# FFN activations and conv's input moved by 64 bytes, FFN and conv products taken by token halves, a separate home for a tail's third weights

## The chip, the cores and the metric

The kernel runs on one core of a Trainium2 chip, in one launch. The metric is the device time of the whole launch in microseconds (us); a value is the median of several executions. A profile of one further execution gives the start and the duration of every instruction on each engine: TensorE (PE, with its weight loads as PEld), VectorE (DVE), ScalarE (ACT), GpSimd (POOL) and SyncE (SP).

## The reference, cut to what matters

A trunk of two layers over 512 tokens of width 1024. Each layer is FFN, mixer, FFN; the first mixer is a gated short convolution, the second a sparse attention. Each of the six sublayers has its own norm with shift, scale and gate.

```python
def adaln(x, g, shift, scale):
    return rms_norm(x, g) * (1 + scale[:, None, :]) + shift[:, None, :]

def swiglu(h, w_in, w_out):                     # D_FF = 2816
    g, u = jnp.split(h @ w_in, 2, axis=-1)
    return (jax.nn.silu(g) * u) @ w_out

def short_conv_mixer(h, w_in, conv_w, w_out):
    b_gate, c_gate, v = jnp.split(h @ w_in, 3, axis=-1)
    u = c_gate * v
    y = lax.conv_general_dilated(u, ...)        # width 3, depthwise, causal
    return (b_gate * y) @ w_out

for i in range(DEPTH):                          # DEPTH = 2
    h = adaln(x, norm_g[i, 0], shift[:, 0], scl[:, 0])
    x = x + HALF * gate[:, 0, None, :] * swiglu(h, ffn_w_in[i, 0], ffn_w_out[i, 0])
    h = adaln(x, norm_g[i, 1], shift[:, 1], scl[:, 1])
    y = short_conv_mixer(...) if i % 2 == 0 else nsa_mixer(...)
    x = x + gate[:, 1, None, :] * y
    h = adaln(x, norm_g[i, 2], shift[:, 2], scl[:, 2])
    x = x + HALF * gate[:, 2, None, :] * swiglu(h, ffn_w_in[i, 1], ffn_w_out[i, 1])
```

## The kernel before

Everything is held transposed: `x[d]` is one block of 128 channels by 512 tokens (d = 0 to 7). Every operand of a matmul is split into a high and a low part, so that a product of one weight block and one block of tokens is three matmuls, in `mm3`: L190 (high weights, high data), L191 (high weights, low data), L192 (low weights, high data). ScalarE rounds a tile to its high part and VectorE subtracts for the low part (`split`, L186 and L187). `HALVES` are the token ranges 0 to 256 and 256 to 512; `HT` is 256.

An FFN (`ffn`, four calls) works through its 22 blocks of the hidden width in four parts (`FOUR`). The input products `gu` are 256 tokens wide: most hidden blocks go through `seven_products`, a scheme with seven instead of eight products on sums and differences of blocks of the input (`th`, `tl`) and of the weights (`qa`, `qb`), whose split weights lie in the pool `sw`. The result of each block is activated and kept as `ahi`, `alo` in the pool `fa` of the class `Hidden`. After each of the first three parts its output products `y` follow: for each d, all blocks of the part, 512 tokens wide (L668), and VectorE adds the result to `x[d]`. The fourth part is the tail: products `ty` by token halves, of six d first, without the last hidden block at first (L695 to L701), then the rest; VectorE adds each to `x` (L408), ScalarE squares it (L271), VectorE sums the squares (L273).

When the sum over all d is complete for a token half, `finish` runs the norm: a small product (L290), `nv` (L292), an inverse square root in ten small VectorE steps `rs_...` (L219 to L233), a diagonal `dg` (L297), and a product that spreads it over the partitions (`pr`, L298). `piece` (L355 to L358) then makes the next layer's input `hhi`, `hlo`, on which the first products of the next layer run (`head_start`, tile `hs`).

The tail's weights are loaded for two d at a time, `ws`, four pairs of tiles: for d = 0 to 3 in the general weights pool (`whi`, `wlo`), for d = 4, 5 and d = 6, 7 in the places of `th2`, `tl2` and of `th0`, `tl0` in the pool `tt`, whose sums are no longer needed.

In `conv` 4 of the 24 blocks of the input product run first, as head start by token halves (`hs`, 192 matmuls); the other 20 are `cv`, 512 tokens wide (480 matmuls).

Where tiles start in on-chip memory is set by the pools: they are stacked from both ends in the order in which they are opened, and `shift(pool, n)` puts n bytes of filler into a pool. The order of instructions on each engine is decided by a scheduler when the program is built, from the order of the code and the priorities (`high_priority`, `issue_after`); an engine then runs its own list in that order.

Of the kernel before, what the change touches and what calls it, by code (L numbers as in the profile page):

```python
# [14 lines left out]
F32R = mybir.dt.float32r  # L15
# [7 lines left out]
P = 128  # L23
D = 1024
T = 512
HT = T // 2
KD = D // P
# [22 lines left out]
HALVES = ((0, HT), (HT, T))  # L50
# [3 lines left out]
def decoder_kernel(ctx, tc, xT, cT, ng, adaw, adab, ffi, ffo, cwi, cw, cwo,  # L54
# [3 lines left out]
    def pool(es, name, bufs, **kw):  # L58
        kw.setdefault("reuse_waits", "tile")
        return es.enter_context(tc.tile_pool(name=name, bufs=bufs, **kw))  # L60


    def shift(p, n):
        p.tile([P, n // 4], F32, name="shift")
# [12 lines left out]
    def psum(name, tag="mm"):  # L77
        tag = next(six) if tag == "mm" else {"pr": "o"}.get(tag, tag)
        return ps.tile([P, T], F32, name=name, tag=tag, bufs=2)
# [36 lines left out]
    for c in range(D // T):  # L116
        o = psum("cb", "nat")
# [3 lines left out]
    def mod(s, kind, d):  # L121
        c = s * NMOD + kind * KD + d
        return mods[:, c:c + 1]
# [65 lines left out]
    def mm3(o, sh, sl, mh, ml, first, last):  # L189
        nc.tensor.matmul(o, sh, mh, start=first, stop=False)  # L190
        nc.tensor.matmul(o, sh, ml, start=False, stop=False)  # L191
        nc.tensor.matmul(o, sl, mh, start=False, stop=last)  # L192

    def weights(src, nk, ncol, own=None, held=3, raws=None, to=None):
        def part(name, dt, bufs, from_):
            return (from_ or wp).tile([P, nk * ncol], dt, name=name, tag=name, padded_shape=[P, KD * P], bufs=bufs)

        held = held if own else 3
        hi, lo = to or (part("whi", F32R, held, own), part("wlo", F32R, held, own))
        raws = raws or own  # L200
        raw = part("wraw", F32, 3 if raws in (None, wp) else 2, raws)
        nc.sync.dma_start(raw.rearrange("p (a n) -> p a n", a=src.shape[1]), src)
        split(raw, hi, lo)
        return [t.rearrange("p (k n) -> p k n", n=ncol) for t in (hi, lo)]


    def project(o, w, wc, h, ks, first, last, a=0, b=T):
        c = slice(wc * P, (wc + 1) * P)
        for n, (kw, k) in enumerate(ks):
            mm3(o, w[0][:, kw, c], w[1][:, kw, c], h[0][k][:, a:b], h[1][k][:, a:b],  # L210
                first and n == 0, last and n == len(ks) - 1)
# [26 lines left out]
    class Halves:  # L238
        def __init__(self, *t):
            self.t = t  # L240
# [226 lines left out]

    class Hidden:
        def __init__(self, es, bufs):
            self.fa = pool(es, "fa", bufs, side="right")  # L470
            self.hi, self.lo = [], []

# [59 lines left out]
    def ffn(s, f, nrm, nxt, w0, ahead, extra=(), soon=()):  # L532
        with ExitStack() as es:
            first = s == 0
            hp = pool(es, "hp", 1)
# [88 lines left out]
                keep(e[:, 0:2].rearrange("p a b -> p (a b)"))  # L624

            js = [(j, c) for j in range(nj) for c in range(2)]
            shift(pool(es, "gap", 1, side="right"), 448)
            tt = pool(es, "tt", 1, side="right")
            if first:
                opening(f, nrm, hid, hp, tt, soon)  # L630
# [4 lines left out]
            else:  # L635
                with ExitStack() as tf_es:
                    nrm.alloc_seven(hp, pool(tf_es, "tf", 1))
                    h = nrm.hi, nrm.lo
                    with ExitStack() as hw_es:
                        hw = pool(hw_es, "hw", 1)  # L640
                        shift(hw, 64)
                        w = w0 + [weights(ffi[f, j, c], KD, P, hw, 1, wp) for j, c in js[len(w0):]]

                        to = [tt.tile([P, D], F32R, name="w" + e, tag=f"t{e}1") for e in "hl"]
# [14 lines left out]
            for p, (j0, j1) in enumerate(FOUR):  # L659
                for j in range(max(j0, nj), j1):  # L660
                    seven_products(j)
                n = j1 - j0
                a = (hid.hi[j0:j1], hid.lo[j0:j1])
                if p < len(FOUR) - 1:
                    for d in range(KD):
                        w = ffn_out(f, d, 1, j0, j1)
                        o = psum("y")
                        project(o, w, 0, a, [(k, k) for k in range(n)], True, True)  # L668
                        added = nc.vector.scalar_tensor_tensor(x[d], o, mod(s, 2, d), x[d], op0=ALU.mult, op1=ALU.add)
                        with tc.issue_after(added.ins):  # L670
                            each()
            assert not todo
            sw_es.close()


            ws = []
            for i, d in enumerate(range(0, KD, 2)):
                if i < 2:
                    ws.append(ffn_out(f, d, 2, j0, j1))
                else:  # L680
                    t = (2, 0)[i - 2]
                    to = [tt.tile([P, KD // 2, HT], F32R, name=f"t{e}{t}").rearrange("p a b -> p (a b)") for e in "hl"]
                    raw = (own if first or i == 2 else quarter[0])().rearrange("p a b -> p (a b)")
                    nc.sync.dma_start(raw.rearrange("p (a n) -> p a n", a=2),
                                      ffo[f, d:d + 2, :, j0 * P:j1 * P].rearrange("d p c -> p d c"))
                    split(raw, *to)
                    ws.append([t.rearrange("p (k n) -> p k n", n=P) for t in to])
# [14 lines left out]
            for d, t in [(d, 0) for d in range(6, KD)] + [(d, HT) for d in range(KD)]:  # L702
                o = psum("ty")
# [6 lines left out]
    def conv(s, nrm, nxt, extra, w0, ahead, own):  # L710
        with ExitStack() as es:
            h_es = es.enter_context(ExitStack())
            hp = pool(h_es, "hp", 1)
            shift(hp, 256)
            ca = pool(es, "cva", 2, side="right")
            h = nrm.alloc(hp)
            ks = [(k, k) for k in range(KD)]
            zh, zl = [], []

            table = bias_table(pool(h_es, "bt", 1))  # L720
            for n in (1, 12, 17):
                extra.insert(n, lambda: next(table, None))
            each = spread(extra, 4 * KD + KD - 3)

            def fill(ins, n):
                with tc.issue_after(ins.ins):
                    for _ in range(n):
                        each()
            for d in range(KD):
                if d == 0:  # L730
                    w = w0 + [weights(cwi[3], KD, P, own)]
                    *os, nx = head_start(nrm, h, [(lambda k, w=w_: (w, 0, k)) for w_ in w])
                else:
                    os = [nx] if d == 1 else []
                    for c in range(len(os), 3):
                        with behind(*nrm.done[0]) if d == 1 else nullcontext():
                            w = weights(cwi[3 * d + c], KD, P, own if (d + c) % 2 else None)
                        o = psum("cv")
                        project(o, w, 0, h, ks, True, True)
                        os.append(o)  # L740
                cg, v, b = os
                cs = tmp("cs")
                nc.scalar.activation(cs, cg, AF.Copy)
                u = ca.tile([P, T + 2], F32, name="u")
                nc.vector.memset(u[:, 0:2], 0.0)
                nc.vector.tensor_mul(u[:, 2:], cs, v)
                y = tmp("yc")
                nc.vector.tensor_scalar(y, u[:, 2:], cws[:, 2 * KD + d:2 * KD + d + 1], None, op0=ALU.mult)
                for i in (1, 0):
                    nc.vector.scalar_tensor_tensor(y, u[:, i:i + T], cws[:, i * KD + d:i * KD + d + 1], y,  # L750
                                                   op0=ALU.mult, op1=ALU.add)
                z = tmp("z")
                nc.vector.tensor_mul(z, y, b)
                hi = ca.tile([P, T], F32R, name="zhi", bufs=KD)
                lo = ca.tile([P, T], F32R, name="zlo", bufs=KD)
                _, rest = split(z, hi, lo)
                zh.append(hi)
                zl.append(lo)
                fill(rest, 4)
            z = (zh, zl)  # L760
            h_es.close()
            tw = pool(es, "tw", 1, side="right")
            for d in range(KD - 3):
                w = weights(cwo[d], KD, P)
                o = psum("y")
                project(o, w, 0, z, ks, True, True)
                fill(residual(s, d, o, nxt), 1)
            assert not extra
            return tail(s, nxt, [(d, weights(cwo[d], KD, P, tw), 0, ks) for d in range(KD - 3, KD)], z, ahead)
# [591 lines left out]
    w = ffn(0, 0, nrm, nxt, None, lambda: [weights(cwi[c], KD, P) for c in range(3)], [small] + late(2), soon)  # L1361
    nrm, nxt = nxt, Norm(2)
    with ExitStack() as ada_es:
        ap = pool(ada_es, "ada", 2)
        home = rows_in(ap)
        w = conv(1, nrm, nxt, [partial(j, home) for j in upto(4, -6)], w, ffn_ahead(1), ap)
    nrm, nxt = nxt, Norm(3)
    w = ffn(2, 1, nrm, nxt, w, ffn_ahead(2), late(5, -3))
    nrm, nxt = nxt, Norm(4)
    w = ffn(3, 2, nrm, nxt, w, lambda: nsa_in(4), late(6))  # L1370
    cd_es.close()
    nrm, nxt = nxt, Norm(5)
    w = nsa(4, nrm, nxt, w, ffn_ahead(3))
# [76 lines left out]
```

## Time and profile before

| | |
|---|---|
| median of 3 runs | 1926.12 us (1925.61 to 1926.36) |
| the profiled execution | 1924.62 us |
| its span | 1922.8 us |
| granted TensorE clock | 1.0 |
| first FFN: tail starts, last `ty` starts | 349.93, 373.27 us |
| second FFN: tail starts | 874.88 us |
| last FFN: tail starts | 1896.17 us |

The span runs from the first to the last instruction that the profile shows; the execution's own time is 1.8 us longer. Times in rows count from the start of the span. A row of the timeline has the start, the duration, the engine, the line of the code, the operation, the tile written and those read, the shapes, a count of instructions that are drawn together, and in brackets how long the engine stood idle before and what ended it. Matmuls are pipelined: a row's duration covers its way through the array, and the next one starts earlier than it ends.

### The profile page before, as it was taken

What the parts mean: (1) busy time and instruction counts of PE and PEld (TensorE: products, weight loads), DVE (VectorE), ACT (ScalarE), POOL (GpSimd) and SP (SyncE); (2) the same over time, 40 slices, a digit from 0 to 9 for tenths busy, and PEclk for the clock granted to TensorE, in tenths of its full rate; (3) what the DMA queues carried; (4) which work ended last, traced back from release to release, by engine and by line L of the source; (5) the groups of instructions that cost most, each with busy time, mean ns of one, the idle gap of its engine ahead of it and who ended that gap; (6) DMA issues with size and microseconds to landing.
All of it is one profiled execution on the core that took longest, in us unless ns stands there. A gap on an engine that the chain in (4) does not pass through costs nothing.

```text
span 1922.8 us, 34307 instructions
## 1 busy us (share of the span) xinstructions
PE 1881.2 (98%) x13321; PEld 1734.8 (90%) x13321; DVE 1584.4 (82%) x2771; ACT 898.7 (47%) x1471; POOL 247.9 (13%) x346
## 2 busy tenths in 40 slices
PE   6999999999999999999999999999999999999999
PEld 4989899988899899999989999999888789898989
DVE  8979888887788798888878888886898988685965
ACT  3435343432245343435634344464787756353532
POOL 0011110000011111110111110000354520010100
PEclk9999999999999999999999999999999999999999
DMA  8587666366656677663667765134322225564731
GB/s 317 193 263 193 217 175 222 124 223 248 227 162 184 210 187 244 173 224 110 173 221 187 230 177 190 63 138 123 98 74 70 89 61 149 153 178 129 187 106 65
DMA packets 126879, 325.07 MB, mean 169 GB/s; under 512 B 15435, under 2 KB 16203, under 8 KB 126716
## 3 DMA queue, kind: packets, MB, share of 16 engines
q1 hardware_dynamic: 95628, 244.13, 37.3%
q0 software_dynamic: 31088, 78.76, 17.8%
q8 instruction: 104, 1.70, 0.3%
q14 instruction: 59, 0.48, 0.1%
HBM read 314.18 MB, written 3.15 MB: 165 GB/s over the span
## 4 chain that ended last, share of the span: by engine, by line
PE 82%; DVE 8%; issue 3%; DMA 3%; POOL 2%; ACT 1%; SPq 1%; DVEq 0%; POOLq 0%; ACTq 0%
PE gu L192 12%; PE gu L190 12%; PE gu L191 12%; PE y L190 7%; PE y L191 6%; PE y L192 6%; PE hs L192 2%; PE hs L191 2%; PE hs L190 2%; PE cv L190 2%; PE cv L191 2%; PE cv L192 2%; PE ty L191 2%; PE ty L192 2%; PE ty L190 2%
## 5 line engine op out<-in xcount | busy, mean ns | idle before, releaser
L186 ACT ACTIVATE whi<-wraw 128x1024 fp32r<-128x1024 f32 (+1 forms) x268 | 262.0, 982 | 397.2 <-PE y L191 188.3
L187 DVE TENSOR_TENSOR wlo<-wraw,whi 128x1024 fp32r<-128x1024 f32 (+1 forms) x268 | 303.3, 1135 | 30.3 <-ACT whi L186 29.6
L190 PE MATMUL y<-ahi,whi 128*128 128x512 f32 x576 | 223.9, 392 | 1.2 <-ACT ahi L186 1.2
L192 PE MATMUL y<-ahi,wlo 128*128 128x512 f32 x576 | 222.8, 390 | 0.6 <-DVE wlo L187 0.6
L191 PE MATMUL y<-alo,whi 128*128 128x512 f32 x576 | 222.9, 390 | 0.0
L141 DVE CUSTOM_DVE_ANT_0 adaraw<-adaraw,cond 128x1024 f32<-128x1024 f32 x144 | 174.0, 1225 | 34.8 <-DMA adaraw<-in_adaw 34.7
L192 PE MATMUL gu<-hhi,wlo 128*128 128x256 f32 x728 | 201.4, 277 | 0.0
L190 PE MATMUL gu<-hhi,whi 128*128 128x256 f32 x728 | 201.4, 277 | 0.0
L191 PE MATMUL gu<-hlo,whi 128*128 128x256 f32 x728 | 201.3, 277 | 0.0
L567 POOL DMA_DIRECT2D qa<-in_ffi x70 | 84.6, 1209 | 691.7 <-DMA qa<-in_ffi 206.2
L192 PE MATMUL gu<-th,qal 128*128 128x256 f32 x584 | 161.4, 276 | 0.7 <-DVE qal L187 0.7
L190 PE MATMUL gu<-th,qah 128*128 128x256 f32 x584 | 161.5, 277 | 0.3 <-ACT p L611 0.3
L191 PE MATMUL gu<-tl,qah 128*128 128x256 f32 x584 | 161.3, 276 | 0.0
L191 PE MATMUL gu<-tl,qbh 128*128 128x256 f32 x584 | 161.3, 276 | 0.0
L192 PE MATMUL gu<-th,qbl 128*128 128x256 f32 x584 | 161.3, 276 | 0.0
L190 PE MATMUL gu<-th,qbh 128*128 128x256 f32 x584 | 161.3, 276 | 0.0
L190 PEld LDWEIGHTS gu<-hhi,whi 128*128 128x128 f32 x728 | 136.7, 188 | 0.5
L191 PEld LDWEIGHTS gu<-hlo,whi 128*128 128x128 f32 x728 | 136.6, 188 | 0.5
L192 PEld LDWEIGHTS gu<-hhi,wlo 128*128 128x128 f32 x728 | 136.7, 188 | 0.1
L186 ACT ACTIVATE qbh<-a 128x512 fp32r<-128x512 f32 x73 | 46.2, 633 | 188.4 <-PE gu L191 172.3
L190 PEld LDWEIGHTS y<-ahi,whi 128*128 128x128 f32 x576 | 107.3, 188 | 27.0 <-ACT ahi L186 5.8
L191 PEld LDWEIGHTS y<-alo,whi 128*128 128x128 f32 x576 | 108.1, 188 | 24.0 <-DVE alo L187 2.2
(320 smaller groups left out, 5602.3 us busy)
## 6 DMA issues: line engine op xcount, KB each, us to landing
wraw<-in_ffi SPq DMA_DIRECT2D x103, 512.0 KB
adaraw<-in_adaw POOLq DMA_DIRECT2D x77, 512.0 KB, 4.4
qa<-in_ffi SPq DMA_DIRECT2D x146, 256.0 KB
wraw<-in_ffo SPq DMA_DIRECT2D x96, 384.0 KB
qa<-in_ffi POOLq DMA_DIRECT2D x70, 512.0 KB, 7.0
adaraw<-in_adaw SPq DMA_DIRECT2D x67, 512.0 KB
a<-in_ffi SPq DMA_DIRECT2D x73, 256.0 KB
wraw<-in_cwi SPq DMA_DIRECT2D x24, 512.0 KB
```

The source lines that it names most:

```text
L141: nc.vector.tensor_tensor_reduce(out=raw, in0=raw, in1=cond, scale=1.0, scalar=0.0, op0=ALU.mult, op1=ALU.add, accum_out=m)
L186: act = nc.scalar.activation(hi, src, AF.Copy)
L187: return act, nc.vector.tensor_tensor(lo, src, hi, ALU.subtract)
L190: nc.tensor.matmul(o, sh, mh, start=first, stop=False)
L191: nc.tensor.matmul(o, sh, ml, start=False, stop=False)
L192: nc.tensor.matmul(o, sl, mh, start=False, stop=last)
L567: nc.gpsimd.dma_start(qa, bass.AP(tensor=a21.tensor, offset=a21.offset, ap=[a21.ap[0], [0, 2], a21.ap[1]]), accum_op=ALU.add)
```

## The change

Four edits. The filler of 448 bytes is put ahead of the pool `fa` instead of behind it, so that `ahi` and `alo` begin 64 bytes into a line of 128, and `tt` stays where it was. The `y` products of d = 1 to 7 are made in two halves of 256 tokens each, that of d = 0 in one as before. The tail's weights for d = 4, 5 get a pool of their own, `held`, on the other side, after `sw` is closed and where its first tiles were; those for d = 6, 7 take the place of `th2`, `tl2`. Conv's input begins 64 bytes into a line of 128 and its `cv` products are made by halves.

```diff
     class Hidden:
         def __init__(self, es, bufs):
+            shift(pool(es, "gap", 1, side="right"), 448)
             self.fa = pool(es, "fa", bufs, side="right")
...
             js = [(j, c) for j in range(nj) for c in range(2)]
-            shift(pool(es, "gap", 1, side="right"), 448)
             tt = pool(es, "tt", 1, side="right")
...
                         o = psum("y")
-                        project(o, w, 0, a, [(k, k) for k in range(n)], True, True)
+                        for t0, t1 in HALVES if d else ((0, T),):
+                            project(o[:, t0:t1], w, 0, a, [(k, k) for k in range(n)], True, True, t0, t1)
...
             sw_es.close()
-
+            es_ws = es.enter_context(ExitStack())
+            held = pool(es_ws, "held", 1)
+            shift(held, 64)
...
                 else:
-                    t = (2, 0)[i - 2]
-                    to = [tt.tile([P, KD // 2, HT], F32R, name=f"t{e}{t}").rearrange("p a b -> p (a b)") for e in "hl"]
+                    if i == 2:
+                        to = [held.tile([P, D], F32R, name="w" + e) for e in "hl"]
+                    else:
+                        to = [tt.tile([P, KD // 2, HT], F32R, name=f"t{e}2").rearrange("p a b -> p (a b)") for e in "hl"]
...
             hp = pool(h_es, "hp", 1)
-            shift(hp, 256)
+            shift(hp, 320)
...
                         o = psum("cv")
-                        project(o, w, 0, h, ks, True, True)
+                        for a, b in HALVES:
+                            project(o[:, a:b], w, 0, h, ks, True, True, a, b)
```

The scheduler orders the engines anew around these edits. Three places follow; names carry the tile numbers of their program.

TensorE in the second FFN, at the start of the first `y` products that follow a part of seven-product blocks; `y_7515` and `y_8504` belong to d = 0, `y_7544` and `y_8533` to d = 1, and `ahi_7505`, `ahi_8494` are the last hidden block of the part. Before:

```order
L192 MATMUL y_7515<-ahi_7380,wlo_7510 128x512
L190 MATMUL y_7544<-ahi_6880,whi_7538 128x512
L191 MATMUL y_7544<-alo_6881,whi_7538 128x512
L192 MATMUL y_7544<-ahi_6880,wlo_7539 128x512
L190 MATMUL y_7515<-ahi_7505,whi_7509 128x512
L190 MATMUL y_7544<-ahi_7005,whi_7538 128x512
L191 MATMUL y_7544<-alo_7006,whi_7538 128x512
L191 MATMUL y_7515<-alo_7506,whi_7509 128x512
```

And after:

```order
L192 MATMUL y_8504<-ahi_8369,wlo_8499 128x512
L190 MATMUL y_8533<-ahi_7869,whi_8527 128x256
L191 MATMUL y_8533<-alo_7870,whi_8527 128x256
L192 MATMUL y_8533<-ahi_7869,wlo_8528 128x256
L190 MATMUL y_8533<-ahi_7994,whi_8527 128x256
L191 MATMUL y_8533<-alo_7995,whi_8527 128x256
L190 MATMUL y_8504<-ahi_8494,whi_8498 128x512
L192 MATMUL y_8533<-ahi_7994,wlo_8528 128x256
```

Between the 15 products of d = 0 on earlier blocks and the first one on the last block stood three matmuls of 512 columns; now five of 256 stand there. The same holds at 11 of the 12 starts of `y` products, all but the first.

TensorE in the second FFN's tail, where its first half turns to the last hidden block (`ahi_9225`, `alo_9226` before, `ahi_10466`, `alo_10467` after). The tiles `ty_9272`, `ty_9273` and `ty_10517`, `ty_10518` belong to d = 0 and 1, `ty_9277` to d = 5, `ty_10520` to d = 3, `ty_10521` to d = 4. Before:

```order
L192 MATMUL ty_9277<-ahi_9100,tl2_9243 128x256
L190 MATMUL ty_9272<-ahi_9225,whi_9230 128x256
L191 MATMUL ty_9272<-alo_9226,whi_9230 128x256
L192 MATMUL ty_9272<-ahi_9225,wlo_9231 128x256
L190 MATMUL ty_9273<-ahi_9225,whi_9230 128x256
L191 MATMUL ty_9273<-alo_9226,whi_9230 128x256
```

And after:

```order
L192 MATMUL ty_10520<-ahi_10341,wlo_10482 128x256
L190 MATMUL ty_10517<-ahi_10466,whi_10475 128x256
L191 MATMUL ty_10517<-alo_10467,whi_10475 128x256
L192 MATMUL ty_10517<-ahi_10466,wlo_10476 128x256
L190 MATMUL ty_10518<-ahi_10466,whi_10475 128x256
L191 MATMUL ty_10518<-alo_10467,whi_10475 128x256
L192 MATMUL ty_10518<-ahi_10466,wlo_10476 128x256
L190 MATMUL ty_10519<-ahi_10466,whi_10481 128x256
L190 MATMUL ty_10521<-ahi_10091,wh_10487 128x256
L191 MATMUL ty_10521<-alo_10092,wh_10487 128x256
```

Six d had their nine matmuls on earlier blocks ahead of that point before, 54 in all; now four have, 36, and the products of d = 4 and 5 with the `held` weights (`wh`) come behind the first products on the last block.

VectorE in the first FFN's tail, from `nv` of the first token half on (`pr_3860`, `pr_4242`). Before:

```order
L292 TENSOR_SCALAR nv_3863<-pr_3860 128x2
L187 TENSOR_TENSOR wlo_3714<-wraw_3715,whi_3713 128x1024
L408 SCALAR_TENSOR_TENSOR x2_84<-ty_3921,mods_117,x2_84 128x256
L273 TENSOR_TENSOR nacc_3789<-nacc_3789,sq_3918 128x256
L219 TENSOR_SCALAR rs_i_3865<-nv_3863 128x2
L408 SCALAR_TENSOR_TENSOR x3_85<-ty_3938,mods_117,x3_85 128x256
L273 TENSOR_TENSOR nacc_3789<-nacc_3789,sq_3935 128x256
L221 TENSOR_SCALAR rs_j_3867<-rs_i_3865 128x2
L224 SCALAR_TENSOR_TENSOR rs_a_3869<-rs_j_3867 128x2
L187 TENSOR_TENSOR wlo_3720<-wraw_3721,whi_3719 128x1024
```

And after:

```order
L292 TENSOR_SCALAR nv_4245<-pr_4242 128x2
L219 TENSOR_SCALAR rs_i_4247<-nv_4245 128x2
L221 TENSOR_SCALAR rs_j_4249<-rs_i_4247 128x2
L224 SCALAR_TENSOR_TENSOR rs_a_4251<-rs_j_4249 128x2
L225 TENSOR_TENSOR rs_b_4252<-rs_a_4251,nv_4245 128x2
L226 SCALAR_TENSOR_TENSOR rs_r0_4253<-rs_b_4252,rs_j_4249 128x2
L408 SCALAR_TENSOR_TENSOR x1_83<-ty_4286,mods_117,x1_83 128x256
L229 TENSOR_TENSOR rs_a_4257<-rs_r0_4253 128x2
L230 TENSOR_SCALAR rs_r1_4259<-rs_r0_4253 128x2
L231 TENSOR_TENSOR rs_b_4258<-rs_a_4257,nv_4245 128x2
L232 SCALAR_TENSOR_TENSOR rs_a_4260<-rs_b_4258 128x2
```

The steps of the inverse square root stood apart, with two weight splits and residuals between the first four of them; now they follow each other, with one residual between.

## The prediction

> **What bounds the kernel now.** First the head of the page, then the chain that ended last.
>
> ```profile
> span 1922.8 us, 34307 instructions
> PE 1881.2 (98%) x13321; PEld 1734.8 (90%) x13321; DVE 1584.4 (82%) x2771; ACT 898.7 (47%) x1471; POOL 247.9 (13%) x346
> PE 82%; DVE 8%; issue 3%; DMA 3%; POOL 2%; ACT 1%; SPq 1%; DVEq 0%; POOLq 0%; ACTq 0%
> ```
>
> TensorE is busy 98% of the span and holds 82% of the chain, so what counts is the distance from one matmul's start to the next and the few places where TensorE waits. The durations in the rows are no distances, since matmuls overlap (a 128x512 one shows 0.39 us and the next starts after 0.23); I read distances from the timeline, as start of the last minus start of the first, over the count. Four places carry the argument. First the first and the last row of 18 steps through one `y` product, then of 84 steps through the `gu` products with `hhi`, and the same 84 in another place:
>
> ```profile
> 204.02 0.39 PE L190 MATMUL y<-ahi,whi 128*128 128x512 f32 x1
> 208.10 0.39 PE L190 MATMUL y<-ahi,whi 128*128 128x512 f32 x1
> 62.73 0.28 PE L190 MATMUL gu<-hhi,whi 128*128 128x256 f32 x1
> 72.25 0.28 PE L190 MATMUL gu<-hhi,whi 128*128 128x256 f32 x1
> 1859.40 0.28 PE L190 MATMUL gu<-hhi,whi 128*128 128x256 f32 x1
> 1868.97 0.28 PE L190 MATMUL gu<-hhi,whi 128*128 128x256 f32 x1
> ```
>
> 4.08 us / 18 = 226.7 ns at width 512; 9.52 / 84 = 113.3 ns at width 256, half of it to 0.1 ns; in the worse place 9.57 / 84 = 113.9 ns. Then the tail of an FFN: 18 steps with the first weights, 11 with the later ones, and conv's head start:
>
> ```profile
> 349.93 0.28 PE L190 MATMUL ty<-ahi,whi 128*128 128x256 f32 x1
> 352.09 0.28 PE L190 MATMUL ty<-ahi,whi 128*128 128x256 f32 x1
> ...
> 371.97 0.28 PE L190 MATMUL ty<-ahi,th 128*128 128x256 f32 x1
> 373.27 0.28 PE L192 MATMUL ty<-ahi,tl 128*128 128x256 f32 x1
> 374.49 0.70 PE L298 MATMUL pr<-dg,ones 128*128 128x256 f32 x2 [0.94 <-DVE u L745]
> 376.30 0.73 PE L190 MATMUL hs<-hhi,whi 128*128 128x256 f32 x4 [0.43 <-ACT hhi L357]
> 376.97 0.38 PE L191 MATMUL hs<-hlo,whi 128*128 128x256 f32 x1
> 400.04 0.40 PE L190 MATMUL cv<-hhi,whi 128*128 128x512 f32 x1
> ```
>
> 2.16 / 18 = 120.0 ns for `ty` on `whi`, 1.30 / 11 = 118.2 ns for `ty` on `th`. From 376.97 to 400.04 TensorE runs the other 188 of the 192 `hs` matmuls and the second half's small norm matmuls (some 0.6 us): 22.5 / 188, about 120 ns. So two kinds of 128x256 matmul of one form differ by 6.7 ns. Adding up the pool sizes in the code, the moving operand starts 64 bytes into a 128-byte line with weights at 0 in the `gu` products (113.3); moving and weights both start at 0 in `ty` on `whi` and in conv's `hs` (120); moving at 0 with weights at 64 is `ty` on `th` (118.2). That is what the change works on.
>
> **The change part by part**
>
> *Tails of the four FFNs (768 `ty` matmuls).* Activations go to 64. 384 matmuls (d = 0 to 3) go from 120.0 to 113.3: 384 x -6.7 = -2.6 us. 192 (d = 4, 5), whose weights now lie in `held` at 0, go from 118.2 to 113.3: -0.9. 192 (d = 6, 7) get weights at 64 against a moving operand at 64, a pair that no row above has; bounded by 113.3 and 120.0, I take the upper, nearest to the 118.2 of these products now: +0.3. Together -3.2 us, -0.8 per tail, if TensorE alone sets the tails. It does not, for two reasons.
>
> Within a tail, the last activation of the part comes while TensorE works on the earlier ones, and the order changes. Before, 54 matmuls on old activations cover its arrival; after, 36 do. In the second FFN, whose tail starts at 874.88:
>
> ```profile
> 874.88 0.28 PE L190 MATMUL ty<-ahi,whi 128*128 128x256 f32 x1
> 878.53 0.69 DVE L187 TENSOR_TENSOR alo<-e,ahi 128x512 fp32r<-128x512 f32 x1 [0.70 <-ACT ahi L186]
> 879.49 1.23 DVE L187 TENSOR_TENSOR wlo<-wraw,whi 128x1024 fp32r<-128x1024 f32 x1 [0.26 <-ACT whi L186]
> 893.95 0.49 DVE L297 TENSOR_SCALAR dg<-ident,rs_r 128x128 f32<-128x128 f32 x2
> 894.49 0.70 PE L298 MATMUL pr<-dg,ones 128*128 128x256 f32 x2
> ```
>
> The last `alo` is ready 4.34 us after the start. After, 36 x 113.3 = 4.08 us and one L190 bring TensorE there at 4.19, and a semaphore later it goes on: about 0.28 us idle. The low half of the `held` weights, on VectorE now behind `alo` and two residuals (L408), is done near 5.7 + 1.23 = 6.9, where TensorE arrives at about 6.75: some 0.16 more. So a tail gets -0.8 + 0.44, about -0.35 net, on TensorE's own account.
>
> Then there is the norm of the next layer. Its first half ends in `dg` (L297), and the broadcast L298 stands in TensorE's queue in front of the last products. In the second FFN `dg` ends at 894.44, 19.56 us into the tail, and L298 follows at once: VectorE, not TensorE, sets that time. VectorE's work ahead of it stays the same, so TensorE arrives earlier and waits. I cost the tails before the third FFN and before the attention at 0, between -0.5 and +0.4.
>
> The last tail has no norm. Its residuals wait for TensorE:
>
> ```profile
> 1917.79 0.48 DVE L408 SCALAR_TENSOR_TENSOR x<-ty,mods,x 128x256 f32<-128x256 f32 x1 [0.93 <-PE ty L192]
> ```
>
> So there the -0.35 reaches the end: -0.3.
>
> *From the first FFN to conv.* Here VectorE's order changes. Before, the chain from `nv` to `dg` is mixed with weight splits and residuals:
>
> ```profile
> 365.55 0.16 DVE L292 TENSOR_SCALAR nv<-pr 128x2 f32<-128x2 f32 x1 [0.30 <-PE pr L290]
> 374.16 0.28 DVE L297 TENSOR_SCALAR dg<-ident,rs_r 128x128 f32<-128x128 f32 x1
> ```
>
> It takes 8.9 us, and L298 comes at 374.49, 1.2 us after the last `ty` (373.27). After, its steps stand almost in a row, with one split and a few residuals between, and I add up VectorE's rows in the new order to `dg` done near 19.4 us into the tail (before: 24.5). L298 then stands before the last 36 `ty`, waits about a microsecond there, and the tail ends near 19.4 + 0.3 + 36 x 0.1133 + 0.3 = 24.1. The first `hlo` needs the residual of the last `ty` and its own operation, 0.48 + 0.48 us and the latencies: `hs` on `hlo` near 25.2 to 25.5, against 376.97 - 349.93 = 27.04. -1.5 us; bounds 0 (VectorE as late as before) and -1.9. The 192 `hs` matmuls then go at 113.3: -1.3, of which I take -1.0, since VectorE and ScalarE must deliver a piece of `h` for each 12 of them. Together -2.5.
>
> *`y` and `cv` by token halves.* 1512 `y` matmuls (7 of 8 d, 3 parts, 4 FFNs, 18 each) become 3024, and 480 `cv` ones 960. 1992 x (2 x 113.3 - 226.7) is 0 by the first rows above; at the worse 113.9, 1992 x 1.1 = +2.2 us; at the 120.0 of the unlucky alignment, +26. I take 0, since these halves have the moving operand at 64 and weights at 0, as the `gu` rows have. What hides the 1992 extra weight loads is that `gu` loads one per 113.3 ns already. The Trainium skill, "TensorE: Matmul & The Clock Gate", section "Back-to-back issue gap", speaks against it: matmul spacing is set by load and matmul together, about 81 ns at N=128 and 131 at N=512, so by a straight line (an estimate) a half would cost 0.75 of a whole and the change +221 us here. The trace disagrees: 113.3 against 226.7 ns is exactly one half.
>
> The 216 `y` matmuls of d = 0 stay 512 wide and now start at 64. No row above shows that; between 0 and 3 ns each, the size of the misses of half a line above, I take 1.5: +0.3.
>
> *Start of each `y` part.* In 11 of the 12 parts the first products run ahead of the last activation:
>
> ```profile
> 717.31 0.39 PE L192 MATMUL y<-ahi,wlo 128*128 128x512 f32 x1
> 717.70 0.73 PE L190 MATMUL y<-ahi,whi 128*128 128x512 f32 x2
> 717.02 0.63 ACT L186 ACTIVATE ahi<-e 128x512 fp32r<-128x512 f32 x1 [0.76 <-DVE e L623]
> ```
>
> `ahi` is ready at 717.65, TensorE waits 0.39 - 0.227 = 0.16 us. Ahead of that wait stand 15 + 3 matmuls of 512 before; after, 15 of 512 and 5 of 256. TensorE gets there 3 x 226.7 - 5 x 113.3 = 113 ns earlier, and what it has not done it does later: 11 x 0.11 = +1.2 us. Nothing hides it: `ahi` hangs on a chain (`gu`, `e`, ScalarE) that does not move.
>
> DMA queues: the tail's weights are as many and as large, GpSimd's order does not change, SyncE's only shifts conv's weight loads by two positions; 0, since no DMA releases TensorE in the rows above.
>
> **The sum**: 0 + 0 - 0.3 - 2.5 + 0 + 0.3 + 1.2 = -1.3 us on the profiled run of 1924.62 (span 1922.8 and 1.8 around it), which lies 1.5 below the median of 1926.12. On the median: 1924.8.
>
> **The rivals**
> - *The tails keep the whole gain* (faster). If VectorE, relieved by nothing but a new order, reaches `dg` earlier everywhere, the two tails at 0 bring the -0.8 of the pitch each and the last one too; the boundary brings -1.5 - 1.3 with its own -0.8, the `y` starts +0.6: -5.4, so 1920.7. For it: VectorE is 82% busy overall and not full. Against it: L298 follows `dg` by 0.05 us at 894.49.
> - *The halves are not free* (slower). Each ns above 113.3 costs 3984 x 1 ns = 4.0 us, so it decides from 0.3 ns (no gain left) and is slower by over 0.2% from 1.3 ns, at 114.6. At 115.4, 2.1 ns above and still less than a third of the way to the 120.0 of the tails, it is +8.4 - 1.3: 1933.2. For it: weight loads are busy 90% and get more. Against: the two quoted stretches of 84.
> - *The `held` weights come late* (slower). If ScalarE's split falls behind one more operation and VectorE's behind another (about 1.0 and 1.2 us), d = 4 waits 2 us in each of four tails: +8 - 1.3, where norms hide part, about 1931.
> - *Alignment is not what makes 120 out of 113* (the change does not do what it says). Then `ty` and `hs` keep their pitch, and the order alone counts: +1.2 at the `y` starts, +0.4 in the last tail, -1.5 at conv: 1926.2. The Trainium skill, "SBUF — State Buffer", section "Who interferes with whom", has TensorE's two read ports independent and knows one contention only, that of VectorE and GpSimd; by it a start address changes nothing. The 6.7 ns between rows of one form speak against it.
>
> **How the numbers follow.** Forecast 0.55, the tails' whole gain 0.20, alignment not the cause 0.10, halves not free 0.08, late weights 0.07. About 0.2% (3.9 us) is what a measurement of this kernel can tell from no change. The forecast and the alignment rival lie within it: 0.65; faster 0.20; slower 0.15. The range goes from the whole gain less the spread of a run, 1920, to the forecast with the worse pitch (+2.2) and the upper bounds of conv (+2.5) and the tails (+0.8): 1930.3.
>
> **What would show it.** A step of 113.3 ns in `ty` on `whi`, in conv's `hs` and in the `y` halves shows the pitch right; 120 in any of them shows it wrong. A gap of some 0.27 us (0.16 before) ahead of the last `ahi` at the `y` starts, and new gaps of 0.2 to 0.4 us in the first half of the tails, would show the waits; L298 waiting for `dg` near 19.5 us into the tails of the second and third FFN would show where the gain went. Wrong it would be if VectorE's chain ends earlier than I add up, or if the weights' second load per product shows in the distances of `y` or `cv`.

## The result, and the profile after

The changed kernel takes 1943.05 us (median of 5 runs, 1940.42 to 1947.05) against 1926.12 us before (5 runs): 1.0093 times the time before, with an interval of 1.0082 to 1.0104. It is slower, by 17 us. Its profiled execution took 1940.42 us. First its page:

```profile
span 1938.3 us, 38297 instructions
PE 1898.3 (98%) x15313; PEld 1832.6 (95%) x15313; DVE 1586.0 (82%) x2771; ACT 897.3 (46%) x1471; POOL 247.9 (13%) x346
PE 78%; DVE 10%; issue 4%; DMA 3%; ACT 3%; POOL 1%; SPq 0%; ACTq 0%; DVEq 0%; POOLq 0%
```

1992 matmuls more, 17 us more in which TensorE is busy, and the same share of the span: it is not waiting more, it is doing the same work more slowly. Setting the first matmul of each stage against that of the same stage before gives the place. The gain or loss of each kind of stage, from the starts in the two timelines:

| stage | us against before |
|---|---|
| 12 `y` parts | +13.4 (eleven of them +1.10 to +1.47; one 0.02, where before had a wait of 1.2) |
| 20 `cv` products | +3.6 |
| conv's head start `hs` | +2.3 |
| first FFN's tail, to the first `hs` | -1.75 |
| second and third FFN's tails | +0.2, +0.1 |
| last tail | -0.2 |
| all else (opening, `gu`, attention) | -2.1 |

The `y` halves then, in the timeline of the changed kernel. In the first part of the first FFN: first and last of 72 steps, a wait for late weights, and first and last of 141 steps behind it; then first and last of 144 steps in the second part:

```profile
99.02 0.28 PE L190 MATMUL y<-ahi,whi 128*128 128x256 f32 x1
...
107.18 0.28 PE L190 MATMUL y<-ahi,whi 128*128 128x256 f32 x1
...
108.46 0.38 PE L192 MATMUL y<-ahi,wlo 128*128 128x256 f32 x1 [0.90 <-DVE wlo L187]
108.69 0.28 PE L190 MATMUL y<-ahi,whi 128*128 128x256 f32 x1
...
125.29 0.28 PE L190 MATMUL y<-ahi,whi 128*128 128x256 f32 x1
...
204.82 0.28 PE L190 MATMUL y<-ahi,whi 128*128 128x256 f32 x1
221.78 0.28 PE L190 MATMUL gu<-hhi,whi 128*128 128x256 f32 x1
```

Before the wait a step takes 8.16 us / 72 = 113.3 ns, behind it 16.60 / 141 = 117.7: the same weights pool, the same activations, one stream. And in the next part 16.96 / 144 = 117.8. Of the 3024 halves 2867 run at 116 to 119 ns, 136 at 115 or less. 813 of the 960 `cv` halves do the same. (2867 + 813) x 4.4 ns = 16.2 us, as much as the whole loss of the profiled execution (1940.42 - 1924.62 = 15.8 us); the other rows of the table nearly cancel out.

The kernel before had it too, in a place that I did not read. The first and the last of 24 steps through the `gu` products that follow a `y` part there:

```profile
220.34 0.28 PE L190 MATMUL gu<-hhi,whi 128*128 128x256 f32 x1
223.17 0.28 PE L190 MATMUL gu<-th,qah 128*128 128x256 f32 x1
```

2.83 / 24 = 117.9 ns for products with the alignment that ran at 113.3 ns in my quoted rows, up to the point where the weights change from `whi` to `qah`. The same stretch stands behind each of the twelve `y` parts there.

The head start of conv, in the changed kernel's timelines of SyncE (with the row of before ahead of them), ScalarE and TensorE:

```profile
360.90 9.62 SPq L202 DMA_DIRECT2D wraw<-in_cwi  x3
```

```profile
369.44 4.74 SPq L202 DMA_DIRECT2D wraw<-in_cwi  x3
374.27 0.38 SPq L139 DMA_DIRECT2D adaraw<-in_adaw  x1
...
377.03 0.42 SPq L139 DMA_DIRECT2D adaraw<-in_adaw  x1
377.49 0.43 SPq L202 DMA_DIRECT2D wraw<-in_cwi  x1
379.69 1.06 ACT L186 ACTIVATE whi<-wraw 128x1024 fp32r<-128x1024 f32 x1 [2.32 <-DMA wraw<-in_cwi]
380.80 0.39 PE L190 MATMUL hs<-hhi,whi 128*128 128x256 f32 x1 [1.59 <-ACT whi L186]
```

Conv's weights are loaded later than before, one block behind two loads for other work, and TensorE waits 1.59 us for their split inside the head start.

### The profile page after: what moved, and what is told of

It is laid out like the page before. It is cut to its first block, busy times and chain, and to the rows that moved or that the text cites. A ratio compares the mean times of both kernels' runs of the same rounds, so it can differ in the third digit from the quotient of the medians.

```text
span 1938.3 us, 38297 instructions
## 1 busy us (share of the span) xinstructions
PE 1898.3 (98%) x15313; PEld 1832.6 (95%) x15313; DVE 1586.0 (82%) x2771; ACT 897.3 (46%) x1471; POOL 247.9 (13%) x346
## 4 chain that ended last, share of the span: by engine, by line
PE 78%; DVE 10%; issue 4%; DMA 3%; ACT 3%; POOL 1%; SPq 0%; ACTq 0%; DVEq 0%; POOLq 0%
PE gu L190 12%; PE gu L191 11%; PE gu L192 11%; PE y L190 6%; PE y L192 6%; PE y L191 6%; PE cv L190 2%; PE cv L192 2%; PE cv L191 2%; PE hs L192 2%; PE hs L191 2%; PE hs L190 2%; PE ty L191 2%; PE ty L192 2%; PE ty L190 2%
## 5 line engine op out<-in xcount | busy, mean ns | idle before, releaser
L190 PE MATMUL y<-ahi,whi 128*128 128x256 f32 (+1 forms) x1080 | 310.0, 288 | 1.7 <-ACT ahi L186 0.8
L192 PE MATMUL y<-ahi,wlo 128*128 128x256 f32 (+1 forms) x1080 | 310.3, 287 | 1.0 <-DVE wlo L187 0.9
L191 PE MATMUL y<-alo,whi 128*128 128x256 f32 (+1 forms) x1080 | 309.3, 287 | 0.0
L190 PEld LDWEIGHTS y<-ahi,whi 128*128 128x128 f32 x1080 | 202.3, 187 | 7.4 <-ACT ahi L186 3.9
L192 PEld LDWEIGHTS y<-ahi,wlo 128*128 128x128 f32 x1080 | 202.8, 188 | 3.7 <-DVE wlo L187 1.4
L191 PEld LDWEIGHTS y<-alo,whi 128*128 128x128 f32 x1080 | 202.7, 188 | 3.2
```

## The experiments

The theories, as far as they could be told apart at that point: P, the pace of a 256-wide stream is fixed by where weights and moving operand lie; L, each further weight load costs 4.4 ns; D, the `y` stage is slowed by what runs beside it; later S, such a stream has two paces and keeps the one it has until something disturbs it. All ratios are to the kernel before, run on the same chip.

**y in one piece** (`y_whole`).

```diff
-                        for t0, t1 in HALVES if d else ((0, T),):
+                        for t0, t1 in ((0, T),):
```

> The changed kernel with the y products of all d in one piece of 512 tokens again; all else as changed (activations 64 into a line, held weights, conv by halves). The trace of the changed kernel puts 12 x 1.16 us on the y parts (117.7 instead of 113.3 ns per half). Every theory of that step expects the step gone: about 1943 - 14 = 1929 us, y at 227 to 230 ns. If the time stays near 1943, the y halves are not where it is lost.

Measured: 1933.0 us, 1.0039 (1.0027 to 1.0052). 10 us are back, not 14: the halves are where most of it is lost, and something else costs some 4 us.

**What is left without halves** (`tails_only`): `y_whole`, and conv as before.

```diff
-                        for a, b in HALVES:
-                            project(o[:, a:b], w, 0, h, ks, True, True, a, b)
+                        project(o, w, 0, h, ks, True, True)
...
-            shift(hp, 320)
+            shift(hp, 256)
```

> The changed kernel with y and cv in one piece and conv's input where it was: what is left of the change is the activations 64 bytes into a line and the held weights. Theory P and theory L alike: no slow halves, the tails' gain as measured (-1.7 us from the first FFN to conv, -0.2 in the last tail, 0 in the others), +0.3 at d = 0 and more for the y products at 512 wide if they run at 227 to 230 ns: 1924 to 1927 us, within 0.2% of before.

Measured: 1931.3 us, 1.0028 (1.0019 to 1.0037): a miss by 4 us and more. The stage starts of its trace say why: the tails gain what they gained (-1.7 to conv), the twelve `y` parts, 512 wide and now with data at 64, take +3.5, of which 1728 x 1.6 ns = 2.7 is the longer step and the rest waits; the `gu` stages behind them +2.5, mostly in steps of 0.38 us, which is one seven-product block of 84 matmuls at 117.8 instead of 113.3; and conv's head start +1.6. So moving the activations costs outside the tails as well.

**Weights at a multiple of 256** (`weights_256`): two small constant tiles move from ahead of the weights pool to behind it.

```diff
-    cws = cst.tile([P, 3 * KD], F32, name="cws")
-    qgs = cst.tile([P, 1], F32, name="qgs")
+    cws = tp.tile([P, 3 * KD], F32, name="cws")
+    qgs = tp.tile([P, 1], F32, name="qgs")
```

> The changed kernel with the general weights pool moved by 128 bytes, so that its tiles begin at a multiple of 256 bytes (they began at 128 over one); nothing else changes place modulo 256, and the y and cv products stay in halves. Theory P (two paces, chosen by the addresses: a stream with weights at 0 modulo 256 returns to 113.3 ns after a wait, one with weights at 128 stays at 117.7): all y halves at 113.3 ns, the half of the cv products that uses this pool too, so about 1943 - 14 - 2 = 1927 us. Theory L (each further weight load costs 4.4 ns): y stays at 117.7 ns, 1943 us. Theory D (the y stage is slowed by what VectorE, ScalarE and the DMAs do beside it): y stays at 117.7 ns, 1943 us.

Measured: 1954.7 us, 1.0145 (1.0127 to 1.0163): slower still. P falls, and so do L and D, since neither sees a reason for a loss here. First and last of 504 steps through the `gu` stage behind the first `y` part, then the start of the next `gu` stage and its end after 504 steps:

```profile
130.45 0.28 PE L190 MATMUL gu<-hhi,whi 128*128 128x256 f32 x1
189.81 0.39 PE L190 MATMUL y<-ahi,whi 128*128 128x512 f32 x1
...
222.93 0.28 PE L190 MATMUL gu<-hhi,whi 128*128 128x256 f32 x1
280.05 0.39 PE L190 MATMUL y<-ahi,whi 128*128 128x512 f32 x1
```

59.36 / 504 = 117.8 ns and 57.12 / 504 = 113.3 ns: two stages of the same products on the same addresses modulo 256, one slow throughout and one fast throughout. Of the 6564 `gu` products with weights at a multiple of 128, 4267 are slow here. Before, the change from `whi` (128 over a multiple of 256) to `qah` (at one) ended the slow stretch after 24 products; where both lie alike nothing ends it. This led to theory S.

**Activations 128 bytes lower** (`acts_128`).

```diff
-            shift(pool(es, "gap", 1, side="right"), 448)
+            shift(pool(es, "gap", 1, side="right"), 320)
...
+            shift(pool(es, "gap2", 1, side="right"), 128)
             tt = pool(es, "tt", 1, side="right")
```

> The changed kernel with the activations 128 bytes lower (64 over a multiple of 256 instead of 192 over it), all else in its place, the weights at 128 over one. If the pace depends on the distance between moving operand and weights modulo 256, which then is that of the fast gu products: y at 113.3 ns, about 1929 us. If it depends on the weights' address alone, or on the number of loads, or on what runs beside: y stays at 117.7 ns, 1943 us.

Measured: 1938.6 us, 1.0060 (1.0043 to 1.0077), between the expectations. Two `y` parts of its trace, first row and the row behind the last half, 243 and 242 steps:

```profile
195.29 0.28 PE L190 MATMUL y<-ahi,whi 128*128 128x256 f32 x1
223.91 0.28 PE L190 MATMUL gu<-hhi,whi 128*128 128x256 f32 x1
...
286.85 0.28 PE L191 MATMUL y<-alo,whi 128*128 128x256 f32 x1
314.27 0.28 PE L190 MATMUL gu<-hhi,whi 128*128 128x256 f32 x1
```

28.62 / 243 = 117.8 and 27.42 / 242 = 113.3 ns. With the operands at this distance the halves fall into either pace, 1102 of 3024 into the slow one: of the 11 parts that begin with a wait four are slow and seven fast. In the changed kernel all 11 are slow. And a wait is not the only thing that drops the pace: behind each of the seven fast parts here the first `gu` product follows without a wait, on other data, and the `gu` run at 117.8 ns from that product on.

**Halves without the move** (`halves_at_0`): the kernel before, `y` by halves and nothing else.

```diff
-                        project(o, w, 0, a, [(k, k) for k in range(n)], True, True)
+                        for t0, t1 in HALVES if d else ((0, T),):
+                            project(o[:, t0:t1], w, 0, a, [(k, k) for k in range(n)], True, True, t0, t1)
```

> The kernel before with one edit: y of d = 1 to 7 in two halves; activations stay at a multiple of 128 bytes. The ty products before, with both operands at a multiple of 128, run at 120.0 ns. If that alignment rules: 1512 x (240.0 - 226.7) = +20 us, 1946 us. If only the further load costs: 3024 x 4.4 ns = +13 us, 1939 us. If halves are free but for the alignment at 64: 1926 us.

Measured: 1944.8 us, 1.0101 (1.0086 to 1.0116), +19 us. First and last of 36 steps, which are the two halves of one d:

```profile
195.76 0.28 PE L190 MATMUL y<-ahi,whi 128*128 128x256 f32 x1
200.08 0.28 PE L190 MATMUL y<-ahi,whi 128*128 128x256 f32 x1
```

4.32 us / 36 = 120.0 ns each step: the price of both operands at a multiple of 128, as forecast. The Trainium skill, "SBUF — State Buffer", "Who interferes with whom", has TensorE's two read ports independent; that the pace hangs on how moving operand and weights lie to each other does not fit this. So the move by 64 was needed for halves; it was not enough.

**No wait ahead of the halves** (`no_wait`), and the same with conv as before (`no_wait_cv`). Of the new code the core:

```diff
+                        prod(d, o, w, range(n - 1 if d < 2 else n))
+                        begun.append((d, w, o))
+                        if d == 0:
+                            continue
+                        for e, w, o in begun:
+                            if e < 2:
+                                prod(e, o, w, range(n - 1, n))
```

> The changed kernel, but in each y part d = 0 and d = 1 are 512 wide and their products on the part's last activation come after the earlier products of both, so that TensorE does not wait for it; d = 2 to 7 in halves as changed. Theory S (a stream of 256-wide products has two paces, 113.3 and 117.7 ns, and keeps the one it has until a wait or a change of alignment disturbs it; it enters y fast and loses that at the wait for the last activation): no wait, so the halves stay at 113.3 ns; 1943 - 14 for the pace - 3 for the waits = 1926 us. Theory L (each further weight load costs 4.4 ns): the halves run at 117.7 ns without a wait too; 1943 - 2 (d = 1 whole) - 3 = 1938 us.

> As no_wait, with the cv products in one piece and conv's input where it was before. Theory S: 3.5 us less than no_wait, from the cv products that ran at 117.7 ns: about 1922 us. Theory L: the same 3.5 us less, from 1938: about 1934 us.

Measured: `no_wait` 1935.5 us, 1.0050 (1.0032 to 1.0067); `no_wait_cv` 1925.4 us, 1.0001 (0.9991 to 1.0011). On the pace S holds: of the 2592 halves 2196 are fast in `no_wait` and 2411 in `no_wait_cv`. The times miss all the same, by 9.5 and 3 us. Against the changed kernel the `y` parts of `no_wait` are 11.5 us shorter, but its `gu` stages 9.0 us longer: TensorE waits there for ScalarE's `p` and for VectorE's splits, up to 1.2 us at a time. Its `cv` halves are nearly all slow (954 of 960), of which the expectation had counted in 813. 10 us lie between the two kernels, where `cv` explains 4. In one `y` part of `no_wait`, 181 halves go at 113.3 ns and the last 33 at 117.8, and between them stands no wait, only two steps of 116 and 121 ns (from 656.88 us on): what tipped it there is not known.

**The same deferral alone** (`defer_whole`): the kernel before, with `y` in one piece, and d = 0 and 1 put off likewise.

> The kernel before with one edit: in each y part the products of d = 0 and d = 1 on the last activation come after the earlier products of both (y stays 512 wide). 11 waits and the uneven steps behind them, 0.33 us each, go: 1926 - 3.6 = 1922.5 us. Rival: the wait comes back elsewhere (the later residuals of d = 0 and 1 hold up VectorE or the result tiles): 1926 us.

Measured: 1928.7 us, 1.0021 (1.0007 to 1.0035): the rival. The trace shows each `y` part 0.33 us shorter, as expected, and the loss behind it:

```profile
672.71 0.39 PE L192 MATMUL gu<-th,qal 128*128 128x256 f32 x1 [1.54 <-DVE qal L187]
```

The last products of d = 0 now stand 15 matmuls of 227 ns later, 3.4 us, and so does its residual on VectorE; the waits in this stage are for VectorE's weight splits and, 0.91 us of them, for ScalarE's `p`. That the one delays the other is inferred: before has one such wait too, of 0.66 us, at the same place of this FFN.

**The wait put back** (`wait_kept`) **and a gentler deferral** (`gentle`). Both are `no_wait_cv` but for the order at the start of a `y` part: `wait_kept` has none of the deferral, `gentle` puts d = 0's last activation behind nine products of d = 1.

```diff
+                        prod(d, o, w, range(n - 1 if gentle and d == 0 else n))
+                        if gentle and d == 0:
+                            w1 = ffn_out(f, 1, 1, j0, j1)
+                            o1 = psum("y")
+                            prod(1, o1, w1, range(3))
+                            prod(0, o, w, range(n - 1, n))
```

> As no_wait_cv, with one difference: the products of d = 0 and d = 1 on the last activation are not put off, so TensorE waits for it again, during products that are 512 wide; the halves of d = 2 to 7 follow the 512-wide ones of d = 1 as there. Theory S (the pace is kept from the last disturbance on, through 512-wide products too): the halves at 117.7 ns, and the gu products behind them until their weights change; 11 x 216 x 4.4 ns = 10.4 us, 11 x 0.3 us of waits, some 0.1 to 0.4 us in each gu stage: about 1925 + 15 = 1940 us. Rival (512-wide products reset the pace, and only a wait among halves matters): halves at 113.3 ns, only the waits come back: 1928 us.

> As no_wait_cv, but only nine products of d = 1 go ahead of d = 0's last activation, and none in the first part of the first FFN, so that VectorE's residual of d = 0 and the weight splits behind it come about 2 us earlier. Theory S: still no wait at the starts, halves and gu at 113.3 ns; and the waits of 0.5 to 1.5 us for late splits in the gu stages of no_wait_cv go: 1920 to 1923 us. If those waits have another cause: 1925 us, as no_wait_cv.

Measured: `wait_kept` 1932.2 us, 1.0036 (1.0022 to 1.0049); `gentle` 1920.2 us, 0.9968 (0.9959 to 0.9977). The same `y` part in both, first half of d = 2 and the row behind the last one, 216 steps; `wait_kept` first:

```profile
196.59 0.28 PE L190 MATMUL y<-ahi,whi 128*128 128x256 f32 x1
222.03 0.28 PE L190 MATMUL gu<-hhi,whi 128*128 128x256 f32 x1
```

```profile
197.70 0.28 PE L190 MATMUL y<-ahi,whi 128*128 128x256 f32 x1
222.18 0.28 PE L190 MATMUL gu<-hhi,whi 128*128 128x256 f32 x1
```

25.44 / 216 = 117.8 against 24.48 / 216 = 113.3 ns. The products, their addresses and the number of weight loads are the same. What differs is the order of the first products of d = 0 and 1, and with it the wait for `ahi`, which stands in `wait_kept` ahead of the halves by 18 products of 512 columns. 2113 of 2592 halves are slow in the one and 172 in the other. In `gentle` 11 of the 12 parts have no wait, and the halves of all 11 are fast. In `wait_kept` these 11 have the wait, and nine are slow; two stay fast behind a wait as long. The weight load that waits, in the `wait_kept` part above and in one of the two that stay at 113.3 ns, and the 216 steps of the latter:

```profile
192.31 0.30 PEld L190 LDWEIGHTS y<-ahi,whi 128*128 128x128 f32 x2 [0.43 <-ACT ahi L186]
...
810.41 0.30 PEld L190 LDWEIGHTS y<-ahi,whi 128*128 128x128 f32 x2 [0.42 <-ACT ahi L186]
...
814.68 0.28 PE L190 MATMUL y<-ahi,whi 128*128 128x256 f32 x1
839.16 0.28 PE L190 MATMUL gu<-hhi,whi 128*128 128x256 f32 x1
```

24.48 / 216 = 113.3 ns again. So taking the wait away keeps the fast pace, and the wait loses it mostly, not always. With that L and D fall for good, since the loads are the same in both and the work beside the stage nearly so. The nine parts at 117.8 ns are 1.25 to 1.55 us longer than in `gentle`, the two at 113.3 ns 0.30, which is the wait alone: 12.4 us in all. The `gu` stages add 1.4, the rest takes off 1.9: 11.9 us between the two profiled executions, 12.1 between the medians. S's expectation of 1940 started from the 1925 of `no_wait_cv`; from the 1920 of `gentle` the same sum gives 1935, and 1.9 less for the two parts that kept the pace. The rival of 1928 falls: 512-wide products do not reset the pace.

`gentle` beats both kernels, the one before by 0.3%, but not because halves are quicker than wholes: a `y` part without the wait takes 32.72 us in it and 32.66 us in `defer_whole`, in one piece. Halves only spare the activations at 64 the 1.6 ns by which a 512-wide product there is longer.

**Conv's part undone alone** (`conv_back`): as in `tails_only`, with `y` by halves kept.

> The changed kernel with conv's part undone alone: input where it was, cv in one piece. From the trace of the changed kernel the cv products cost 3.6 us more by halves and conv's head start 2.3 us more (a wait for weights, 1.6 us of it). If both belong to conv's part: 1943 - 5.9 = 1937 us; if the head start's wait stays: 1943 - 3.6 = 1939.5 us.

Measured: 1942.9 us, 1.0088 (1.0072 to 1.0103), not to be told from the changed kernel. The trace has the `cv` stage back at the length of before and the head start still 2.3 us longer, so that wait does not come from conv's edit. The 3.6 us of `cv` do not show in the time. Against the trace of the changed kernel the `gu` stages are 2.4 us longer here, seven of them by 0.36 us, which is one block of 84 more at the slow pace; and the profiled run carries a single wait that no other trace here has at this place, so this run does not settle the size of conv's part:

```profile
196.33 0.51 PE L190 MATMUL y<-ahi,whi 128*128 128x512 f32 x1 [3.86 <-ACT ahi L186]
```

## Why the prediction was wrong

**The step that failed** is the one on `y` and `cv` by token halves: "I take 0, since these halves have the moving operand at 64 and weights at 0, as the `gu` rows have." Alignment opens the pace of 113.3 ns; it does not hold it. After a wait the same stream mostly runs at 117.7 ns and goes on so, and the `y` parts begin with a wait in 11 of 12 cases; all 11 were slow, and where `gentle` has no wait, all 11 were fast. The term was not 0 but some 16 us, between my two ends (0 and +26) and far from the one I took. The rows that I quoted for 113.3 came from the middle of `gu` stages; the 24 products behind each `y` part, at 117.9, were in the same trace. One of my quoted stretches even held the end of such a one: "the worse place" at 113.9 ns is 12 steps at 117.8 and 72 at 113.3. At 512 columns a step is 226.7 ns before such a wait and behind it, as the long rows of `y` before showed, so the old form carried no such risk. For the `cv` halves it is inferred: their slow stretch begins behind the wait in conv's head start, but no run takes that wait away and keeps them in halves.

**The rival that came true** is "the halves are not free", to which I gave 0.08 and a price of 2 ns where 4.4 came. Its mechanism as I had it, the further weight load, was not the cause: `gentle` has the loads and not the loss. The Trainium skill's rule ("TensorE: Matmul & The Clock Gate", "Back-to-back issue gap"), which would have put the halves far above half of a whole, is not borne out either: a half took 113.3 or 117.7 ns, a whole 226.7.

**SyncE's order.** "SyncE's only shifts conv's weight loads by two positions; 0" was wrong. Before, the row of conv's weight loads begins 11.0 us into the tail (360.90 - 349.93), now 17.7 us (369.44 - 351.77), and ScalarE's split, TensorE's operand, waits for one of them. Whether SyncE's order alone delays them or also a buffer that comes free later was not separated. The head start was to gain 1.0 and lost 2.3, more than the tail ahead of it had won; 1.59 of it is this wait. Its products did not go at the 113.3 ns forecast either, but at 117.8 (126 steps from 387.58 to 402.42 us): the same step of the prediction failed here too.

**The tails** came out as worked out. From the first FFN to conv -1.75 (forecast -1.5), with `dg` here ending at 371.33, 19.6 us into the tail (19.4):

```profile
370.85 0.48 DVE L297 TENSOR_SCALAR dg<-ident,rs_r 128x128 f32<-128x128 f32 x2
371.38 0.48 PE L298 MATMUL pr<-dg,ones 128*128 128x256 f32 x1
```

The second and third FFN's tails +0.2 and +0.1 (forecast 0, the norm taking the gain), the last -0.2 (-0.3). Alignment does rule the tail's pace where no wait disturbs it: the first 36 `ty` of a tail go at 113.3 ns, those of d = 6, 7, with weights and data both at 64, at 120.

**The starts of the `y` parts**: the wait did grow, by about 0.11 us each as worked out:

```profile
191.09 0.28 PE L190 MATMUL y<-ahi,whi 128*128 128x256 f32 x1
191.21 0.28 PE L191 MATMUL y<-alo,whi 128*128 128x256 f32 x1
191.86 0.50 PE L190 MATMUL y<-ahi,whi 128*128 128x512 f32 x1 [0.38 <-ACT ahi L186]
```

From 191.21 to 191.86 is 0.65 us, less a step of 0.11: this one is 0.54 us. Nine of the eleven stand at 0.27, where before had 0.16. What I did not see is that the wait also sets the pace of the 247 halves behind it.

**The 216 `y` of d = 0**: 1.6 ns each by `tails_only`, 1.5 forecast. That was the middle of a range from 0 to 3, so the match is luck.

**A row that I read wrongly.** The 118.2 ns of `ty` on `th` I took for the price of data at 0 and weights at 64. By the pool sizes the attention's tail has the same pair in `ohi` and `ehhi`, and the trace of before shows it at the fast pace, first and last of 60 steps:

```profile
1561.68 0.28 PE L190 MATMUL ty<-ohi,ehhi 128*128 128x256 f32 x1
1568.48 0.28 PE L190 MATMUL ty<-ohi,ehhi 128*128 128x256 f32 x1
```

6.80 / 60 = 113.3 ns. So 118 was the slow pace here too, and one more sign of two paces on one alignment that lay in the trace of before.

What stays open is why a wait drops the stream into the slow pace at most places and not at all of them (11 of 11 in the changed kernel, 9 of 11 in `wait_kept` at the same addresses, 4 of 11 in `acts_128`), and what the hardware does in it; the runs show only when it happens.

## What to carry to other kernels

The pace of a matmul stream is read not from one stretch but from stretches with different things ahead of them: behind a wait, behind wider products, behind a change of tiles. Whoever splits wide products into narrow ones should first take the wait out of the stage's start, and then look at what the wait's removal makes late on the engine that drains the results. An order changed by a scheduler moves loads too: a load that is issued some us later is a term of the sum.

## What the runs showed of the hardware

Products of 128x256 in fp32r whose moving operand and weights lie 64 bytes apart modulo 128 have two lasting paces, 113.3 and 117.8 ns a matmul (`y` in `gentle` and in `wait_kept`; `ty` on `ehhi` and on `th` before). With both at a multiple of 128 (`halves_at_0`), or both at 64 (the last `ty` of a tail in the changed kernel), there is one of 120.0. The pace lasts over changes of tile and over products of 512 columns between (`wait_kept`), for 504 products in a row and more (`weights_256`). Behind a wait it fell to the slow one in 20 of 22 parts at the changed kernel's addresses (11 of 11 there, 9 of 11 in `wait_kept`); a change of operands without a wait did it too (`acts_128`). In the kernel before, the slow stretch behind each of the twelve `y` parts ended where the weights changed from 128 over a multiple of 256 to a multiple of it; in `wait_kept` it did so in four of nine parts, and in the other five one block of 84 products later.
